# Queues, PSUM banks, tile places and the last block's weights, changed in a one-core encoder layer

## The chip, the core and the metric

The kernel runs on one NeuronCore of a Trainium2 chip. Five engines work beside each other, each through its own instructions in order: TensorE (PE in the profile; its weight loads are PEld), VectorE (DVE), ScalarE (ACT), GpSimd (POOL) and SyncE (SP), which here only issues DMAs. ACT and POOL can issue DMAs as well. The metric is the device time of one execution in microseconds.

## The reference

One inference step of a one-layer encoder in float32, for 2048 prompt tokens and 32 sample tokens, D_MODEL = 1024, D_FF = 4096:

```python
n = rmsnorm(x);  z = n @ w_in
A = sliding-window attention with sinks (8 heads of 64, window 128, chunks of 64)
B = gated linear attention (4 heads, dk 64, dv 128, state carried over chunks)
h = x + concat(A, B) @ w_out
y = h + relu(rmsnorm(h) @ w_up)**2 @ w_down
```

Outputs are y for both token sets, the last keys and values, and the GLA states.

## The kernel before

Every float32 operand is split into a high and a low float32r half, and a product is three matmuls (`mm3`: high by high, high by low, low by high). Tokens lie along the free axis, transposed, in chunks of 128.

**Attention** runs over 16 chunks and leaves its output of each chunk in a DRAM buffer `mixT` (the `aT` stores). **GLA** (gated linear attention) runs over the same chunks two at a time, with decay products `E` on POOL from a table `cc`, and puts its half into `mixT` (the `gT` stores). **The out-projection** (`op_phase`) takes the 2080 tokens as three pieces p of two groups gi, of 328 or 356 tokens a group: for each of eight feature blocks f, `op<-mx..,wo..` sums into PSUM, DVE adds the residual (tile y{p}{gi}, L1274), squares go into `acc` (L1277), and a matmul with ones (`oprb`) brings the token norm. The mix of a group is loaded from `mixT` and split into `mx0h`, `mx0l` or, for every other group, `mx1h`, `mx1l`.

**The FFN** is done by a Strassen-Winograd scheme: the matrices are cut in 2x2 quarters, and seven products take the place of eight. Its operands are sums of quarters. For tokens these are B11, B21, B22, T1 to T4, made by `post` in `op_phase` after a piece's second group and kept in DRAM as `Td`. For weights they are A11, A12, A22, S1 to S4, split in pairs on the fly by ACT (high) and DVE or POOL (low, L1380). The quarter sums of `w_down` (`sd`) are made by POOL in the phases before (L712) and stored: a unit is a load from `w_down`, some additions in place, and a store. EARLY blocks are made in the attention phase, in 4 parts each, in the two `cc` tiles that GLA uses later; MIDDLE blocks in GLA, the rest in `op_phase`. The three pieces run in the order 1, 2, 0. A piece has 16 blocks b of 256 of the 4096 features; a block has seven up steps (U, PSUM `u`) and seven down steps (D, PSUM `dn`), the D steps lagging behind the U steps, and the results are gathered in seven accumulators P1 to P7. The first piece also stores the sums of `w_up` (`su`) and the pairs of the first and last block (`ku`, `kd`), which the later pieces load. `prepare` makes weight pairs six steps ahead (AHEAD).

At a change of piece, the next piece's seven token operands are loaded and split, `load_tok`: a DMA into the low tile, ACT copies the high half, DVE or POOL subtract. These DMAs are ACT's; all others are SP's (queue Q, L59).

The order on each engine comes from a scheduler that runs over generators; their `yield n` are times on an estimated PE clock, which says when a piece of side work is offered. Each engine then runs its list in order. PSUM has eight banks: through the out-projection three for `oprb`, `opa`, `opb` and five for products; in the FFN, `ps2` holds two tiles of two banks for `dn`, and `ps1` the rest for `u`.

The lines that the prediction touches:

```python
S.dma_start(f32(l), self.Td[e.p][x])                       # load_tok
self.Q.dma_start(raw[:, k], w[b, :, k, :, c0 : c0 + n])    # load_block
Q.dma_start(self.mixT[t][:, 4:8, :], gT[:, :, :L])         # gla_phase
```

## Time and profile before

| | |
|---|---|
| Time, median of 3 runs | 2291.27 us (2290.83 to 2297.01) |
| Time of the profiled execution | 2295.51 us |
| Its span | 2293.6 us |
| Mean granted clock of TensorE | 0.968 |
| Busy: PE, DVE, ACT, POOL | 2155.3, 1575.3, 1232.0, 1474.0 us |
| Moved by DMA | 372.65 MB, 162 GB/s in the mean |

The phases in the profile: attention up to about 378 us, GLA to 745, the out-projection to 947, then the pieces of the FFN to about 1410, 1860 and the end. Busy time is read against what ended the idle time before an instruction: in `idle <-releaser` the releaser is the instruction or DMA whose semaphore came last. "SPq" and "ACTq" are the DMA issues of an engine's instruction list. PEclk is the TensorE clock that was granted, 1.00 being full speed.

### The profile page before, as it was taken

What the parts mean: (1) busy time and instruction counts of PE and PEld (TensorE: products, weight loads), DVE (VectorE), ACT (ScalarE), POOL (GpSimd) and SP (SyncE); (2) the same over time, 40 slices, a digit from 0 to 9 for tenths busy, and PEclk for the clock granted to TensorE, in tenths of its full rate; (3) what the DMA queues carried; (4) which work ended last, traced back from release to release, by engine and by line L of the source; (5) the groups of instructions that cost most, each with busy time, mean ns of one, the idle gap of its engine ahead of it and who ended that gap; (6) DMA issues with size and microseconds to landing.
All of it is one profiled execution on the core that took longest, in us unless ns stands there. A gap on an engine that the chain in (4) does not pass through costs nothing.

```text
span 2293.6 us, 40613 instructions
## 1 busy us (share of the span) xinstructions
PE 2155.3 (94%) x14790; PEld 2021.7 (88%) x14790; DVE 1575.3 (69%) x3442; ACT 1232.0 (54%) x2728; POOL 1474.0 (64%) x1324
## 2 busy tenths in 40 slices
PE   7999999799998599789999998999999989999997
PEld 6777777687887599789999998999999989999996
DVE  8766666688886445657777775576666666676667
ACT  4545455455563122456666665665565556666662
POOL 5233345343452453658878779978887889888884
PEclk9999999799998799899999999999999999999999
DMA  8344564251434875744444348544443475445433
GB/s 272 132 147 138 184 200 151 85 188 63 150 116 130 301 263 210 272 163 141 133 133 136 128 136 290 162 132 142 141 140 123 149 255 165 153 141 155 149 109 120
DMA packets 212729, 372.65 MB, mean 162 GB/s; under 512 B 43297, under 2 KB 140882, under 8 KB 207282
## 3 DMA queue, kind: packets, MB, share of 16 engines
q1 hardware_dynamic: 209506, 355.16, 47.0%
q10 hardware_dynamic: 3024, 14.91, 1.8%
q8 instruction: 116, 1.90, 0.3%
q14 instruction: 83, 0.68, 0.1%
HBM read 275.03 MB, written 94.98 MB: 161 GB/s over the span
## 4 chain that ended last, share of the span: by engine, by line
PE 52%; DMA 2%; DVE 2%; ACT 0%; issue 0%; POOL 0%; SPq 0%; ACTq 0%; DVEq 0%
PE dn L156 26%; PE u L156 26%; DVE P L1498 1%; DMA T3l<-Td2T 0%; DMA T1l<-Td2T 0%; DMA T1l<-Td0T 0%; DMA T2l<-Td0T 0%; DMA T3l<-Td0T 0%; DVE u L1498 0%; DMA B21l<-Td0B 0%; DMA T2l<-Td2T 0%; DVE P L1598 0%; SPq L59 0%; DMA stage<-sd 0%; DMA B11l<-Td2B 0%
## 5 line engine op out<-in xcount | busy, mean ns | idle before, releaser
L1498 DVE TENSOR_TENSOR P<-P,dn 128x712 f32<-128x712 f32 (+1 forms) x642 | 559.7, 875 | 234.5 <-PE dn L156 217.4
L43 ACT ACTIVATE u<-u 128x356 f32<-128x356 f32 (+1 forms) x384 | 174.0, 453 | 39.9 <-PE u L156 22.3
L43 ACT ACTIVATE r<-u 128x356 f32<-128x356 f32 (+1 forms) x192 | 88.6, 461 | 135.7 <-PE u L156 135.7
L1498 DVE TENSOR_TENSOR u<-u,r 128x356 f32<-128x356 f32 (+1 forms) x144 | 75.7, 526 | 122.5 <-PE u L156 117.6
L712 POOL TENSOR_TENSOR sd<-sd 128x128 f32<-128x128 f32 (+2 forms) x144 | 107.5, 761 | 75.1 <-DMA sd<-in_w_down 66.1
L945 POOL TENSOR_TENSOR E<-cc 128x256 f32<-128x256 f32 (+1 forms) x117 | 69.5, 628 | 103.2 <-DVE cc L797 49.0
L1405 POOL TENSOR_TENSOR stage<-stage 128x512 f32<-128x512 f32 x92 | 119.3, 1298 | 13.8 <-DMA stage<-in_w_up 8.3
L1021 DVE COPY_PREDICATED AT<-masks,A 64x64 f32<-64x64 int32 (+1 forms) x330 | 82.8, 253 | 22.3 <-ACT AT L43 13.0
L1598 POOL TENSOR_TENSOR P<-P,P 128x712 f32<-128x712 f32 (+1 forms) x38 | 65.0, 1732 | 21.8 <-DVE P L1498 21.6
L1274 DVE TENSOR_TENSOR y<-op,y 128x356 f32<-128x356 f32 (+1 forms) x48 | 23.5, 516 | 79.1 <-PE op L156 50.8
L43 ACT ACTIVATE P<-S,negm 128x192 f32<-128x192 f32 (+2 forms) x128 | 51.6, 417 | 46.7 <-DVE negm L577 38.4
L43 ACT ACTIVATE E<-E 128x1024 f32<-128x1024 f32 (+2 forms) x68 | 67.4, 1013 | 1.4 <-POOL E L937 0.3
L595 POOL TENSOR_TENSOR P<-P,es 128x512 f32<-128x512 f32 x15 | 16.0, 1065 | 74.2 <-ACT sq L43 44.4
L43 ACT ACTIVATE op<-y 128x356 f32<-128x356 f32 (+1 forms) x42 | 18.7, 464 | 76.0 <-DVE y L1274 67.6
L845 POOL TENSOR_TENSOR g<-g,ggla 128x512 f32<-128x512 f32 (+1 forms) x17 | 23.1, 1373 | 48.6 <-ACT g L43 48.6
L1498 DVE TENSOR_TENSOR u<-u,f 128x356 f32<-128x356 f32 (+1 forms) x96 | 49.9, 519 | 5.8 <-ACT u L43 5.7
L43 ACT ACTIVATE pS<-pT 128x256 f32<-128x256 f32 (+1 forms) x62 | 27.4, 490 | 48.9 <-PE pT L160 48.8
L956 DVE TENSOR_TENSOR E<-E,kq 128x256 f32<-128x256 f32 (+1 forms) x117 | 51.5, 496 | 1.5 <-ACT E L43 1.2
L576 DVE TENSOR_REDUCE mx<-S 128x2 f32<-128x384 f32 (+2 forms) x64 | 32.7, 535 | 28.6 <-PE S L156 28.4
L43 ACT ACTIVATE v<-go 128x256 f32<-128x256 f32 (+1 forms) x34 | 12.7, 380 | 73.5 <-DVE Sp L1053 46.0
L1281 POOL TENSOR_TENSOR z<-y 128x356 f32<-128x356 f32 (+1 forms) x12 | 11.8, 983 | 53.0 <-DVE y L1274 35.0
L43 ACT ACTIVATE f<-u 128x356 f32<-128x356 f32 (+1 forms) x96 | 43.7, 455 | 0.0
(1913 smaller groups left out, 8867.9 us busy)
## 6 DMA issues: line engine op xcount, KB each, us to landing
stage<-in_w_up SPq DMA_DIRECT2D x92, 512.0 KB, 3.9
stage<-sd SPq DMA_DIRECT2D x92, 512.0 KB, 4.4
stage<-in_w_down SPq DMA_DIRECT2D x46, 512.0 KB, 3.6
stage<-su SPq DMA_DIRECT2D x30, 512.0 KB, 3.9
stage<-in_w_down SPq DMA_DIRECT2D x46, 256.0 KB, 3.0
sd<-in_w_down SPq DMA_DIRECT2D x22, 512.0 KB, 5.6
sd<-sd SPq DMA_DIRECT2D x11, 1024.0 KB, 5.1
xT1a<-in_xT_prompt SPq DMA_DIRECT2D x16, 512.0 KB, 4.5
```

The lines of the kernel that those rows point to most:

```text
L43: ins = f(*args, **kw)
L156: self._pe(self.T.matmul(out, lhsT, rhs, start=start, stop=stop, **kw), ns)
L576: V.reduce_max(mx[:, ch, us], sp, axis=AX.X)
L712: self.G.tensor_tensor(out=o, in0=x, in1=y, op=op)
L845: G.tensor_tensor(out=gv, in0=gv, in1=ggla[:r].unsqueeze(1).broadcast_to([r, 4, P]), op=ALU.mult)
L945: G.tensor_tensor(out=e4, in0=c4, in1=ref, op=ALU.subtract)
L956: V.tensor_tensor(out=e4, in0=e4, in1=halves_of(kq, L, m), op=ALU.mult)
L1021: V.copy_predicated(dst, mk.unsqueeze(1).broadcast_to([L // nh, 2, w // m, m]), src[r].rearrange("s p (n m) -> s p n m", m=m),)
L1274: V.tensor_tensor(out=y[:, f], in0=ps, in1=y[:, f], op=ALU.add)
L1405: tt = lambda o, x, y, op: G.tensor_tensor(out=o, in0=x, in1=y, op=op)
L1498: add = lambda out, x, y, op=ALU.add: V.tensor_tensor(out=out, in0=x, in1=y, op=op)
L1598: eng.tensor_tensor(out=e.acc[q][:, j : j + 2], in0=e.acc[q][:, j : j + 2], in1=e.acc[x][:, j : j + 2], op=ALU.add)
```

## The change

Seven edits come together.

1. **Queues.** The stores of attention and GLA outputs, of the residual y and of the token operands go from SP's queue to ACT's, which makes their data last. The loads and stores of the weight sums, and the stores of kept sums and kept weight pairs, go from SP to POOL (G). The token loads go from ACT to SP; for the first piece five of the seven stay on ACT. The last piece's token stores stay on SP, cut in three by yields over the first four D steps.
2. **Token combinations.** `post` uses the PSUM tiles `rb` and `A` only; `B` is gone. The products of the out-projection get six banks. The FFN's `ps2` is cut in two pools, and the first four D steps of its first block use only the second, which does not lie over `rb` and `A`.
3. **Aligned tiles.** Paddings and the order of pools change, so that FFN tiles come to lie on single tiles of the out-projection: B11's high half on `mx0h`, the accumulators on y20, y21, z and the sums' tiles.
4. **EARLY** is 4 where it was 5; `op_phase` now makes seven blocks of sums.
5. **The last block's down pairs** are made and stored in blocks 9 to 12 of the first piece (`keep_last`), no longer in block 15. In block 14 the two pairs that DVE made are POOL's.

The core of the diff:

```diff
-EARLY, MIDDLE = 5, 5
+EARLY, MIDDLE = 4, 5
+PAD1, PADX = 164, 600
...
-                Q.dma_start(self.mixT[t][:, 4:8, :], gT[:, :, :L])
+                S.dma_start(self.mixT[t][:, 4:8, :], gT[:, :, :L])
...
-            self.Q.dma_start(raw[:, k], w[b, :, k, :, c0 : c0 + n])
+            self.G.dma_start(raw[:, k], w[b, :, k, :, c0 : c0 + n])
...
+            self.G.dma_start(self.sd[b][:, :, c0 : c0 + n], raw.rearrange("p k m n -> p (k m) n"))
             yield 6000
-            with self.tc.issue_after(self.Q.last.ins):
-                self.Q.dma_start(self.sd[b][:, :, c0 : c0 + n], raw.rearrange("p k m n -> p (k m) n"))
-            yield 8000
...
-            self.Q.dma_start(dst, x)
+            self.G.dma_start(dst, x)
...
+        pr, pp = pool("opr", 1, space=PSUM), pool("opp", 6, space=PSUM)
+        rb, pa = (pr.tile([P, 512], F32, tag=x, name=f"op{x}") for x in ("rb", "a"))
...
             for k in range(H):
                 scaled(A, k)
+                tt(y[:, k], A, y0[:, k])
                 scaled(y[:, H + k], H + k)
-                tt(t3[:, k], y[:, H + k], A)
-                tt(A, A, y0[:, k])
-                S.activation(y[:, k], A, AF.Copy)
-                tt(B, y[:, H + k], A)
-                S.activation(y0[:, k], B, AF.Copy)
-                tt(y0[:, H + k], y0[:, H + k], B)
+                tt(A, y[:, H + k], A)
+                S.activation(t3[:, k], A, AF.Copy)
+                tt(A, A, y0[:, k], ALU.add)
+                S.activation(y0[:, k], A, AF.Copy)
+                tt(y0[:, H + k], y0[:, H + k], A)
...
-            amem = {i: mem(pool(f"acc{i}"), H * NM, f"P{i}", F32) for i in (3, 5, 7, 6, 2, 4, 1)}
             umem["T4"] = upair(pool("ud"), "T4")
+            amem = {i: mem(pool(f"acc{i}"), H * NM, f"P{i}", F32) for i in (5, 7, 6, 2, 4, 1, 3)}
...
+            def keep_last(part):
+
+                b = NF - 1
+                if part == 0:
+                    s = load(w_dn[b, :, 0:1, :512], True)
+                    weights(f"d{b}A11", s, True, G)
+                    return
+                s = load(w_dn[b, :, 1:2, :] if part == 3 else self.sd[b][:, 2 * (part == 1) : 2 * (part == 1) + 2], True)
+                names = (("S4", "S1"), ("S2", "S3"), ("A12", "A22"))[part - 1]
+                cut = (s[:, :, :512], s[:, :, 512:]) if part == 3 else (s[:, 0:1], s[:, 1:2])
+                for x, src in zip(names, cut):
+                    weights(f"d{b}{x}", src, True, G)
...
-            def load_tok(e, x, engs):
+            def load_tok(e, x, engs, queue=Q):
 
                 h, l = e.T[x]
-                S.dma_start(f32(l), self.Td[e.p][x])
+                queue.dma_start(f32(l), self.Td[e.p][x])
...
-                    ps = ps2.tile([P, 2, 512], F32, tag="two", name=f"dn{g}_{q}_{j}")
+                    two = ps2[1] if g == 0 and i < 4 else ps2[j // 2]
+                    ps = two.tile([P, 2, 512], F32, tag="two", name=f"dn{g}_{q}_{j}")
...
+                    if n == 0 and 9 <= b < 13 and i == 3:
+                        keep_last(b - 9)
```

SP's list at the start of the out-projection, before (y01, y10 and y00 are residual tiles, `mixT` the mix, 128x8x40 is partitions by feature blocks by tokens):

```order
L59 DMA mixT15_81<-gT_15_9080 128x512
L59 DMA sd9_145<-sd9_0_8552 128x2048
L59 DMA y10_9263<-in_xT_prompt 128x8x128
L59 DMA y10_9263<-in_xT_prompt 128x8x84
L59 DMA y01_9214<-in_xT_prompt 128x8x88
L59 DMA y01_9214<-in_xT_prompt 128x8x128
L59 DMA y01_9214<-in_xT_prompt 128x8x112
L59 DMA m_4_112_9316<-mixT4_70 128x8x16
L59 DMA m_5_0_9320<-mixT5_71 128x1024
L59 DMA y00_9200<-in_xT_prompt 128x8x128 x2
L59 DMA y00_9200<-in_xT_prompt 128x8x40
L59 DMA y00_9200<-in_xT_sample 128x8x32
```

The loads of y00 are the last of the three residual tiles, behind the last `gT` store. After the change, SP's list in the middle of GLA (nTb, caf and g are loads of the next chunks of GLA):

```order
L60 DMA nTb_4h_5960<-nTh8_91 128x2048
L60 DMA nTb_4l_5961<-nTl8_92 128x2048
L60 DMA y00_9175<-in_xT_prompt 128x8x128
L60 DMA caf_4_6456<-ca8_109 96x128
L60 DMA g_7_6081<-rgd7_126 128x512
L60 DMA caf_4_6456<-ca9_110 96x128
L60 DMA y00_9175<-in_xT_prompt 128x8x128
L60 DMA y00_9175<-in_xT_prompt 128x8x40
L60 DMA y00_9175<-in_xT_sample 128x8x32
L60 DMA g_8_6615<-rgd8_127 128x512
L60 DMA rb_5_6485<-rs_118 128x128 x2
```

The loads of y00 moved from behind the last rows of GLA, and behind y10 and y01, to between the loads of the fourth pair of chunks.

DVE's list at the start of the FFN, before (opa and opb are the PSUM tiles of `post`, P3 and P5 accumulators, dn results of D steps):

```order
L1209 SCALAR_TENSOR_TENSOR opa_9198<-y21_10304,packed_211,oprb_9197 128x356
L1209 SCALAR_TENSOR_TENSOR y21_10304<-y21_10304,packed_211,oprb_9197 128x356
L1220 TENSOR_TENSOR y20_9883<-y20_9883,opb_9199 128x356
L1498 TENSOR_TENSOR uT4l_10827<-u0_0_10914,uT4h_10826 128x356
L1220 TENSOR_TENSOR T32_10718<-y21_10304,opa_9198 128x356
L1220 TENSOR_TENSOR opa_9198<-opa_9198,y20_9883 128x356
L1220 TENSOR_TENSOR opb_9199<-y21_10304,opa_9198 128x356
L1220 TENSOR_TENSOR y20_9883<-y20_9883,opb_9199 128x356
L1592 COPY P3_10798<-dn0_3_0_11169 128x712
L1592 COPY P3_10798<-dn0_3_2_11177 128x712
```

Both evacuations of P3 stand behind all of the combinations. After the change, the same list:

```order
L1220 TENSOR_TENSOR y20_9858<-y20_9858,opa_9146 128x356
L1615 COPY P3_10813<-dn0_3_0_11151 128x712
L1210 SCALAR_TENSOR_TENSOR opa_9146<-y21_10282,packed_211,oprb_9145 128x356
L1210 SCALAR_TENSOR_TENSOR y21_10282<-y21_10282,packed_211,oprb_9145 128x356
L1220 TENSOR_TENSOR y21_10282<-opa_9146,y20_9858 128x356
L1220 TENSOR_TENSOR opa_9146<-y21_10282,opa_9146 128x356
L1615 COPY P3_10813<-dn0_3_2_11159 128x712
L1390 TENSOR_TENSOR wf_d0A12_11215<-stage_11169,wf_d0A12_11215 128x512
L1220 TENSOR_TENSOR opa_9146<-opa_9146,y20_9858 128x356
```

The first evacuation by DVE, of P3, stood behind all combinations; it now stands ahead of the last one, and the second inside it.

More of the change, by code (lines that the diff above doesn't have):

```diff
@@ L1161, in op_phase @@
         nt, H = self.nt, KB // 2
+        pr, pp = pool("opr", 1, space=PSUM), pool("opp", 6, space=PSUM)
+        rb, pa = (pr.tile([P, 512], F32, tag=x, name=f"op{x}") for x in ("rb", "a"))
         m1 = pool("opm1", 1)
-        mem1 = [m1.tile([P, KB * REST + 272], F32R, tag=x, name=f"mx1{x}") for x in "hl"]
+        mem1 = [m1.tile([P, KB * REST + PAD1], F32R, tag=x, name=f"mx1{x}") for x in "hl"]
         m0 = pool("opm0", 1)
         mmem = [[m0.tile([P, KB * REST], F32R, tag=x, name=f"mx0{x}") for x in "hl"], mem1]
-        yps = [pool(f"opy{i}", 1) for i in (1, 2)]
-        tp, sp, xp = pool("opt", 1), pool("ops", 2), pool("opx", 3)
-        yps.insert(0, pool("opy0", 1))
+        sp, tp = pool("ops", 2), pool("opt", 1)
+        yps = [pool(f"opy{i}", 1) for i in (2, 1)]
+        xp = pool("opx", 3)
+        yps = [pool("opy0", 1), *yps[::-1]]
         stage = lambda name, n: tp.tile([P, H * REST], F32, tag="t", name=name)[:, : H * n].rearrange("p (k t) -> p k t", k=H)
-        rb, pa, pb = (self.ps_m(x) for x in ("oprb", "opa", "opb"))
         g = lambda f: self.gffn[:, f : f + 1]
@@ L1214, in post @@
                 yield
[L1215 to L1216 removed]
+                S.dma_start(Td["B11"], y[:, :H])
+                S.dma_start(Td["B21"], y[:, H:])
                 return
[L1218 to L1220 removed]
+            A, y0 = pa[:, :N], ys[p, 0]
+            tt = lambda o, x, z, op=ALU.subtract: V.tensor_tensor(out=o, in0=x, in1=z, op=op)
             for k in range(H):
                 scaled(A, k)
+                tt(y[:, k], A, y0[:, k])
                 scaled(y[:, H + k], H + k)
[L1224 to L1232 removed]
+                tt(A, y[:, H + k], A)
[3 more added lines that the diff above has]
+                tt(y0[:, H + k], y0[:, H + k], A)
+            last = p == 2
+            yield
+            eng = Q if last else S
+            eng.dma_start(Td["T3"], t3)
+            if last:
+                yield
+            eng.dma_start(Td["T1"], y[:, :H])
+            eng.dma_start(Td["B22"], y[:, H:])
+            if last:
+                yield
+            eng.dma_start(Td["T2"], y0[:, :H])
+            eng.dma_start(Td["T4"], y0[:, H:])
         mix = {(0, gi): self.mix[gi] for gi in range(2)}
@@ L1244, in begin @@
         def begin(b):
-            x = xp.tile([P, 2592], F32, tag="x", name=f"sd{b}")[:, :2048].rearrange("p (k m n) -> p k m n", k=2, m=2)
+            x = xp.tile([P, 2048 + PADX], F32, tag="x", name=f"sd{b}")[:, :2048].rearrange("p (k m n) -> p k m n", k=2, m=2)
             self.load_block(x, b, 0, 512)
@@ L1255, in end @@
         def end(b):
-            Q.dma_start(self.sd[b], sums.pop(b)[0].rearrange("p k m n -> p (k m) n"))
+            G.dma_start(self.sd[b], sums.pop(b)[0].rearrange("p k m n -> p (k m) n"))
         load_y(0, 0)
@@ L1268, in op_phase @@
                 else:
-                    ps = self.ps_s(f"op{p}_{gi}_{f}")[:, :N]
+                    ps = pp.tile([P, 512], F32, tag="op", name=f"op{p}_{gi}_{f}")[:, :N]
                     cs = slice(f % H * P, f % H * P + P)
@@ L1305, in ffn_phase @@
             pool = lambda name, **kw: ctx.enter_context(tc.tile_pool(name=name, bufs=kw.pop("bufs", 1), **kw))
-            ps2, ps1 = pool("ps2", bufs=2, space=PSUM), pool("ps1", space=PSUM)
+            ps2 = [pool(f"ps2{x}", space=PSUM) for x in "ab"]
+            ps1 = pool("ps1", space=PSUM)
             w_dn = a["w_down"].rearrange("(b k p) n -> b p k n", k=2, p=P)
@@ L1312, in ffn_phase @@
             tmem = tok(pool("toka"), ("T2", "T1"))
-            upair = lambda pool, x: [mem(pool, NM, f"u{x}{y}") for y in "hl"]
+            upair = lambda pool, x: [mem(pool, NM + 12 * (x + y == "B21h"), f"u{x}{y}") for y in "hl"]
             rf = pool("rf")
@@ L1465, in down_weights @@
                         src["A12"], src["A22"] = s[:, :, :512], s[:, :, 512:]
-                    eng = V if n == 0 and i in (0, 5) and not keep else G
-                    out[x] = weights(f"d{b}{x}", None if made else src[x], keep, eng)
+                    eng = V if n == 0 and i in (0, 5) and b < NF - 2 else G
+                    out[x] = weights(f"d{b}{x}", None if made else src[x], False, eng)
                     yield
@@ L1628, in ffn_phase @@
             for x, t in UP:
-                load_tok(envs[0], t, (V, G))
+                load_tok(envs[0], t, (V, G), Q if t in ("B11", "B21") else S)
             ups = {}
```

24 lines of the change are left out of this document (8 added, 16 removed).

## The prediction, made before the changed kernel ran

> **What bounds the kernel now.** I began with the busy shares and the clock row of the page.
>
> ```profile
> PE 2155.3 (94%) x14790; PEld 2021.7 (88%) x14790; DVE 1575.3 (69%) x3442; ACT 1232.0 (54%) x2728; POOL 1474.0 (64%) x1324
> PEclk9999999799998799899999999999999999999999
> ```
>
> TensorE (PE) is busy for 2155.3 of 2293.6 us, so 138 us of the span are idle on it. The change removes no matmul and keeps PE's order. It can only win idle time, and the part of the busy time that ran at a lowered clock. The waits of PE say where the idle time lies.
>
> ```profile
> PE oprb L156 <- issue: 21.1, 1, 21.1
> PE dn L156 <- DVE P L1498: 19.2, 9, 6.2
> PE dn L156 <- DVE y L1220: 13.1, 1, 13.1
> PE go L156 <- ACT cc L43: 9.8, 1, 9.8
> PE u L156 <- ACT B11h L43: 5.9, 1, 5.9
> PE op L156 <- POOL mx0l L1114: 5.8, 1, 5.8
> PE op L156 <- ACT mx0h L43: 2.9, 1, 2.9
> PE u L156 <- ACT r L43: 2.0, 1, 2.0
> PE dn L156 <- POOL wf_d0S L1380: 1.9, 1, 1.9
> PE u L156 <- DVE B11l L1496: 1.6, 1, 1.6
> ```
>
> (Columns: total us, times, longest.) They cluster at five joints: the start of GLA (`go`), of the out-projection (`oprb`, `op`), of the FFN (`u`, then `dn` behind `y`), and the two changes of piece. Inside a piece there is nothing to win. Each joint also lowers the clock behind it, which the windows show (columns after the name: length, then busy us of PE, PEld, DVE, ACT, POOL; PEclk; DMA share; GB/s).
>
> ```profile
> 421.00:430.00 9.00, 8.71 (x50) 6.67 (x51) 4.89 (x15) 7.90 (x17) 3.89 (x6) 0.52 0.17 46
> 771.00:778.00 7.00, 6.28 (x27) 6.31 (x28) 2.58 (x13) 0.00 (x0) 6.73 (x6) 0.51 0.88 315
> 800.00:812.00 12.00, 5.42 (x18) 5.18 (x19) 0.50 (x1) 4.15 (x7) 12.00 (x9) 0.57 0.86 255
> 947.00:959.00 12.00, 9.77 (x35) 8.90 (x36) 6.63 (x9) 4.73 (x8) 11.24 (x7) 0.51 1.02 418
> 982.00:987.00 5.00, 4.40 (x17) 4.43 (x18) 0.45 (x1) 1.36 (x2) 0.00 (x0) 0.59 1.02 418
> 1407.00:1413.00 6.00, 5.53 (x19) 5.53 (x20) 4.71 (x8) 3.86 (x8) 6.00 (x5) 0.52 0.75 298
> 1842.00:1847.00 5.00, 4.79 (x20) 4.79 (x21) 2.14 (x3) 0.16 (x1) 5.00 (x4) 0.66 0.92 359
> 1853.00:1857.00 4.00, 3.96 (x15) 3.50 (x15) 3.37 (x7) 3.42 (x8) 2.63 (x2) 0.57 1.05 411
> ```
>
> Busy time times (1 - clock) is what the clock cost: 4.2, 3.1, 2.3, 4.8, 1.8, 2.7, 1.6 and 1.7 us in turn. A joint's worth is its idle time plus this.
>
> **Start of GLA: 9.8 + 4.2 = 14.0 us.**
>
> ```profile
> 419.62 2.06 POOL L712 TENSOR_TENSOR sd<-sd 128x128 f32<-128x128 f32 x4 [1.93 <-DMA sd<-in_w_down]
> 420.39 0.84 ACT L43 ACTIVATE cc<-la,packed 128x256 f32<-128x256 f32 x2 [12.57 <-DMA sd<-sd]
> ```
>
> ACT cannot write `cc` until a store of early sums has left the same memory: the fifth early block is still being summed at 419.6. With EARLY at 4 no such block exists, and its work becomes a GLA unit with tiles of its own. I take 12 of the 14, since that unit now sits on POOL before the second group of decay products.
>
> **Start of the out-projection: 21.1 + 3.1 = 24.2 us.** PE stands before `oprb`, the token norm of group (0,0). DVE and SP tell why.
>
> ```profile
> DVE y L1274 <- DMA m<-mixT: 18.5, 1, 18.5
> DVE y L1274 <- DMA y<-in_xT_sample: 6.0, 1, 6.0
> 734.97 0.61 SPq L59 DMA_DIRECT2D mixT<-gT  x1
> 736.10 10.09 SPq L59 DMA_DIRECT2D y<-in_xT_prompt  x5
> ...
> 749.19 3.75 SPq L59 DMA_DIRECT2D y<-in_xT_prompt  x3
> 752.98 1.62 SPq L59 DMA_DIRECT2D y<-in_xT_sample  x1
> L1277 DVE TENSOR_TENSOR acc<-acc,op 128x328 f32<-128x328 f32 x8 | 9.8, 1236 | 0.6
> L1277 DVE TENSOR_TENSOR acc<-acc,op x42: 489/525/1375, 761.2 to 942.6; 128x356 f32<-128x356 f32 x28, 128x328 f32<-128x328 f32 x14
> ```
>
> The residual tile that group (0,0) adds to (y00) is loaded last, up to 752.98, behind the last `gT` store and the loads of two other groups. After the change its rows stand in GLA, and the `gT` stores are on ACT's queue. DVE can then finish the group as its products arrive. What stays is the `acc` chain: eight additions that took 1.24 us each here, between 745 and 780, against a median of 0.525 over all 42, while POOL made its sums. I leave 6 us of the 24.2 and take 18.
>
> The same stage then waits 2.9 + 5.8 us for `mx0h` and `mx0l` (worth 11.0 with the clock). Those loads still come off SP, DMA is 0.86 to 0.88 busy there, and POOL now issues 13 transfers ahead of the first `mx0l`. I take nothing.
>
> **Start of the FFN.** B11's tile (128544 to 134240 in a partition) lay over `mx1l`, the low half of the last group's mix; its new place is `mx0h`, free one group earlier. So 5.9 + 1.6 us idle and 4.8 of clock go: 12.3, of which I take 12. Next, `dn` waits 13.1 us because its banks were those of the combinations, and DVE finishes these first. In the change the first four down steps use one other buffer of two banks, so the first runs at once. Two prices stand against that. The third down result is evacuated by DVE in program order, behind three of the four combinations; and in one combination a PSUM tile serves where two did, so DVE waits for ACT's copies more often.
>
> ```profile
> L1220 DVE TENSOR_TENSOR opa<-opa,y x12: 501/532/533, 824.4 to 979.8; 128x356 f32<-128x356 f32 x8, 128x328 f32<-128x328 f32 x4
> L43 ACT ACTIVATE y<-opa x4: 467/468/477, 965.4 to 980.4; 128x356 f32<-128x356 f32 x4
> ```
>
> Two DVE subtractions hang on two ACT copies of 0.47 us each combination, some 1.0 us with the round trip left out, four times. DVE is late by 4 us there, and the single buffer costs an evacuation of under 1 us per step. I leave 8 of the 13.1, keep the clock loss, and take 5. From both sides: 13 if DVE is ahead, nothing if it isn't.
>
> **Changes of piece.** Here ACT issues each token load when its own order comes to it, and then stands still for the landing.
>
> ```profile
> 1392.21 0.80 ACT L43 ACTIVATE T1h<-T1l 128x712 fp32r<-128x712 f32 x1 [6.43 <-DMA T1l<-Td2T]
> 1392.22 0.36 ACTq L43 DMA_DIRECT2D T3l<-Td2T  x1
> 1400.56 1.49 ACT L43 ACTIVATE T3h<-T3l 128x712 fp32r<-128x712 f32 x2 [3.81 <-DMA T3l<-Td2T]
> 1332.00:1357.00 25.00, 25.00 (x156) 25.00 (x155) 19.64 (x29) 15.90 (x34) 19.42 (x16) 1.00 0.30 99
> 1382.00:1408.00 26.00, 17.16 (x103) 16.61 (x102) 12.16 (x19) 14.19 (x29) 26.00 (x18) 0.96 0.88 313
> ```
>
> Moving these loads to SP takes the 6.43 and 3.81 us out of ACT. Seven weight pairs of the last block and their stores leave the stretch 1382 to 1408, where POOL has no free time, for blocks 9 to 12, where it was busy 19.42 of 25 us. At the first change the waits are 2.65 and 6.2 (of the 19.2 above) and 1.9, with 2.7 of clock: 13.4, and I take 9. At the second they are 2.0, 2.85 and 1.17, with 3.3 of clock: 9.3, and I take 5, since no weights move there. SP now carries those loads among its weight loads; a load that waits for its tile holds the weights behind it, which is why I don't take all.
>
> **The issues themselves.** ACT's DMAs go from 21 to 64. At the 0.36 us of the rows above the 43 more take 15 us, spread over 950 us of an engine that is 54% busy, and behind work that the store needs anyway; I count nothing. Should ACT be late in GLA, where its order feeds the next chunk, these 15 us would be the most.
>
> 116 issues move to POOL. The trace of before has none from POOL, so I bound one: from below by ACT's 0.36 us, the same kind of instruction; from above by a whole transfer, since issuing cannot take longer than issue to landing.
>
> ```profile
> sd<-in_w_down SPq DMA_DIRECT2D x22, 512.0 KB, 5.6
> L1405 POOL TENSOR_TENSOR stage<-stage 128x512 f32<-128x512 f32 x92 | 119.3, 1298 | 13.8 <-DMA stage<-in_w_up 8.3
> ```
>
> The tightest place is blocks 9 to 12: 19.4 us of work in 25, plus 7/4 pairs of 1.30 us (2.3), plus 2.75 issues. At 0.36 us that is 22.7 us and nothing is late. At 2 us it is 27.2, and 4 x 2.2 = 9 us pile up, which the lead of six weight steps (6/14 of a block, 10.7 us) still hides. I take the low end, as the kind of instruction is the same, and 3 us for sums that now wait in POOL's order for loads issued just before them. The far end, 5.6 us, is a rival below. Block 14's two pairs that go from DVE to POOL (2.6 us) take the room that block 15's leave.
>
> The Trainium skill, page "SBUF — State Buffer", section "A bandwidth-pool intuition that's wrong (but worth ruling out)", says that a transfer issued from GpSimd takes about 0.62 us alone and 3.1 us beside a DVE copy that locks their shared port. No run here shows it yet. By 3.1 us the four blocks would be at 30.2 us, 21 us late in all, and the time some 17 us longer than my sum.
>
> **Sum.** 12 + 18 + 0 + 12 + 5 + 9 + 5 - 3 = 58 us. The profiled execution took 2295.5 us, which gives 2237.5. It lies 4.2 above the median 2291.27 of the runs shown (2290.83 to 2297.01), so for a median I forecast 2235 us.
>
> **Rivals.**
>
> *Half the joints stay* (22%). At the out-projection the transfers themselves may be the bound: DMA is at 0.88 there, and the tiles of four groups still have to arrive; at the FFN's start DVE's order holds `dn` as before. Then only GLA (12), B11 (12) and the changes of piece (14) pay: 38, less 3, so about 2257. Against it: the y00 rows move by a whole phase.
>
> *The wait moves into GLA* (8%). Row y00 on SP now waits until POOL has stored block 8's sums, and the next chunks' `caf` and `g` loads are queued behind it. If POOL gets there late, SP stalls in GLA and PE loses about what it won at the out-projection, 18 us with the clock: about 2253.
>
> *POOL's issues are dear: slower* (10%). The place is POOL before `mx0l` and in blocks 9 to 12, and c is the time of an issue.
>
> ```profile
> L712 POOL TENSOR_TENSOR sd<-sd 128x512 f32<-128x512 f32 x12 | 16.8, 1421 | 31.6 <-DMA sd<-in_w_down 31.4
> ```
>
> Between 745 and 780 POOL idles 31.6 us, so 13 issues are covered up to c = 2.4. In the four blocks the lag is 4 x (19.4 + 2.3 + 2.75c - 25), less 10.7 us of lead (six of the 14 steps of a 25 us block). At c = 4 these are 20 and 20 us, with about 12 of clock and as much again where early units crowd the attention phase; that eats the 58. From about 4 us an issue the kernel is slower; at 5 it is 33 + 31 + 14 + 20 - 58 = 40 us over, about 2335. Against it: POOL's issue would be ten times ACT's.
>
> The skill's figure of 3.1 us would fall short of that point.
>
> *Gains and costs cancel* (5%): c between 3 and 4, about 2288.
>
> **How the numbers follow.** The forecast, 55%, is 2235, with its own range 2215 to 2257 (every joint paid in full would be 2205). The range for 8 in 10 goes from 2207 to 2288. A measurement of this kernel tells 0.3%, 7 us, from no change. Faster: 55 + 22 + 8 = 85%, and 1 of the cancelling case, 86%; same 5%; slower 9%.
>
> **What would show it.** `go` no longer waits for `cc`; `oprb` waits under 8 us and DVE has no `y` wait for the sample rows; `u` has no wait for `B11h`; `dn` behind `y` is 8 us or less, with P3's evacuation as releaser; ACT has no wait of over 2 us for T1l or T3l. Idle PE time should fall from 138 to about 95 us. I am wrong if waits of PE for POOL's `E`, `P` or `wf_d` of blocks 9 to 13 grow, or if `op` waits longer for `mx0l` than 8.7 us.

## The result, and the profile after

| | before | after |
|---|---|---|
| Time, median of 20 runs | 2295.3 us | 2280.64 us |
| Ratio to before, 95% interval | 1 | 0.994 (0.9923 to 0.9957) |
| Span of the profiled execution | 2293.6 us | 2271.6 us |
| PE idle in it | 138 us | 116 us |

The kernel became faster by 0.6%, 14.7 us in the medians; the forecast was 58. One run of the kernel before took 2655.74 us, in a slower state, and is not in the ratio. The profiled execution of the changed kernel, 2273.34 us, is one of its faster ones, so its profile shows 22 us of gain.

The waits of PE after the change (total us, times, longest) have new entries in place of the old ones.

```profile
PE dn L157 <- DVE P L1520: 14.4, 9, 3.5
PE dn L157 <- DVE P L1615: 13.1, 4, 7.0
PE op L157 <- DVE y L1283: 8.3, 1, 8.3
PE go L157 <- ACT kdT L44: 6.8, 1, 6.8
...
PE op L157 <- POOL mx0l L1113: 4.7, 1, 4.7
PE oprb L157 <- DVE rsq_y_y L248: 4.4, 1, 4.4
PE op L157 <- ACT mx0h L44: 3.9, 1, 3.9
```

The waits for `cc`, for `oprb` at the start of the out-projection and for `B11h` are gone, 36.8 us in all. Each of the first four rows and the sixth holds something the forecast did not have.

PE runs the same list of matmuls in every version of this document, so the start of one matmul can be compared between profiles. The table gives, at the matmul that began at t in the profile before, how much later (+) or earlier (-) a version began it. The steps between columns are where a version wins or loses.

```text
t before (us)       120    400    460    540    740    785    940    970   1010   1270   1345   1450   1830   1910    end
after             +10.4   +3.4  -12.0   -7.9  -18.0  -41.3  -22.9  -39.1  -24.7  -25.1  -13.4  -22.6  -22.2  -24.7  -23.8
e1_no_keep        +11.8   +5.5   -7.8   -0.5  -10.3  -33.5  -12.4  -26.5  -10.1  -10.4  -10.6   -4.2   -4.8   -5.7   -4.6
e2_b11_pool        +9.6   +2.1  -13.7   -6.1  -16.9  -40.1  -18.0  -38.2  -24.1  -24.5  -13.4  -21.3  -21.5  -21.5  -20.6
e3_a_pool         +10.4   +4.9   -8.7   -4.2  -14.6  -37.5  -16.0  -31.7  -13.4  -13.8  -12.8  -17.8  -17.7  -17.1  -16.3
e4_tok_act         +8.8   +2.4  -11.2   -7.2  -16.9  -40.1  -19.6  -33.7  -17.1  -17.5   -7.9  -11.9  -12.6   -8.7   -8.6
e5_mid7            +8.7   +0.9  -13.5   -9.6  -16.3  -39.2  -25.5  -45.7  -29.2  -29.6  -21.2  -22.2  -22.2  -27.7  -27.7
e6_early5         +10.3   +1.2  -13.9   -9.5  -15.5  -38.8  -25.0  -39.1  -22.7  -23.1  -13.9  -17.8  -18.2  -20.1  -19.9
e7_sums_sp         +1.5   -4.6  -21.2  -26.0  -18.7  -39.4  -20.8  -38.4  -21.7  -22.1  -19.6  -29.8  -30.5  -30.9  -30.7
e8_no_align        +8.5   +2.6  -11.7   -4.8  -13.1  -36.3  -25.6  -37.3  -15.1  -15.1   -4.5   -3.5   -2.6   -3.4   -2.6
e9_comb            -0.0   -6.6  -20.0   -8.7  -10.1  -33.3  -20.1  -34.8  -20.8  -21.2  -19.6  -26.4  -27.1  -28.1  -27.2
e10_early_sp       +1.8   -5.7  -20.8   -8.7  -19.6  -42.4  -20.9  -34.0  -15.5  -15.9   -6.2  -11.4  -12.1  -13.8  -13.6
e11_late_y00      +12.4   +4.7  -11.1  -13.3  -24.5  -42.2  -21.0  -35.7  -21.9  -22.3  -12.4  -17.5  -18.2  -20.6  -20.4
e12_ps2            +9.8   +4.4   -9.3   -3.1  -13.8  -36.6  -14.6  -21.7  -20.9  -21.3  -11.0  -13.1  -13.8  -19.6  -19.4
e13_three          +1.3   -6.0  -21.0  -20.4  -32.3  -49.6  -34.0  -49.0  -35.7  -36.1  -35.5  -40.8  -40.4  -44.9  -44.7
e14_early5_three   +1.7   -3.9   -4.3   -3.8  -12.9  -32.3  -14.4  -28.0  -11.5  -11.9  -12.2  -17.4  -18.1  -18.8  -17.9
e15_no_es          +8.4   +2.1  -11.8  -11.5  -22.3  -39.7  -24.9  -37.2  -22.4  -22.8  -21.8  -24.3  -23.8  -24.9  -24.7
```

Row "after" in steps: 10 us lost at the start of attention and mostly regained by 400; 15 won at the start of GLA (400 to 460); 4 lost and 10 won inside it (460 to 540, 540 to 740); 23 won at the start of the out-projection (740 to 785) and 18 lost inside it (785 to 940); 16 won and 14 lost again at the start of the FFN; 12 lost in blocks 11 and 12 of the first piece (1270 to 1345); 9 won and 2 won at the changes of piece. Four places gave back what the joints had won. One lies in each of the next four timelines.

Each row is one execution, so a step is only as sure as it repeats. Up to 1214 us the lists of all engines are the same in "after", e1, e3 and e4, whose edits touch later blocks only. These four win 22.8 to 23.3 us at the start of the out-projection and lose 18.4 to 21.5 inside it, but from 940 to 1010 one wins 1.8 and three lose 2.3 to 2.6, and at 940 their sums stand 10 us apart.

**Blocks 11 and 12.** DVE, then POOL, then PE, in the changed kernel:

```profile
1267.19 0.88 DVE L1520 TENSOR_TENSOR P<-P,dn 128x712 f32<-128x712 f32 x1
1267.99 6.12 DVE L1390 TENSOR_TENSOR wf_d11A<-stage,wf_d11A 128x512 fp32r<-128x512 f32 x1
1274.47 1.68 DVE L1520 TENSOR_TENSOR P<-P,dn 128x712 f32<-128x712 f32 x2
...
1267.34 1.28 POOL L1390 TENSOR_TENSOR wf_d11S<-stage,wf_d11S 128x512 fp32r<-128x512 f32 x1
1268.59 1.27 POOL L1390 TENSOR_TENSOR wf_u12S<-stage,wf_u12S 128x512 fp32r<-128x512 f32 x1
1269.83 1.27 POOL L1415 TENSOR_TENSOR s<-stage 128x512 f32<-128x512 f32 x1
1271.07 1.27 POOL L1390 TENSOR_TENSOR wf_u12S<-stage,wf_u12S 128x512 fp32r<-128x512 f32 x1
1272.31 1.25 POOL L1415 TENSOR_TENSOR stage<-stage 128x512 f32<-128x512 f32 x1
...
1275.41 0.43 PE L157 MATMUL dn<-uT3h,wf_d11S 128*128 128x356 f32 x1 [3.33 <-DVE P L1520]
```

A subtraction that takes 0.68 us elsewhere (both operands in SBUF) lasts 6.12 us, until half a microsecond after POOL's gapless run ends at 1273.6. The accumulation behind it is late, and PE waits. Block 12 shows the same at 1300. The accumulations `P<-P,dn`, with one operand in PSUM, are not slowed beside POOL.

**Inside the out-projection**, DVE waits for a residual tile. The window (columns as in the prediction's) shows the DMA engines full meanwhile (share 1.05, 353 GB/s).

```profile
833.89 2.70 DVE L1283 TENSOR_TENSOR y<-op,y 128x356 f32<-128x356 f32 x6 [15.40 <-DMA y<-in_xT_prompt]
800.00:832.00 32.00, 26.17 (x167) 25.87 (x166) 7.33 (x23) 3.25 (x5) 14.91 (x11) 0.96 1.05 353
```

**At the FFN's start** the first `dn` no longer waits long, but the third accumulator's evacuation waits for a store: P5's new place is the tile of T3.

```profile
964.37 0.90 DVE L1615 COPY P<-dn 128x712 f32<-128x712 f32 x1 [3.83 <-DMA Td2T<-T]
956.48 0.93 SPq L60 DMA_DIRECT2D Td2T<-T  x1
```

**In GLA**, SP waits 10.2 us for a store of sums before it can load y00, and GLA's own `g` load is queued behind; ACT then waits for `g`.

```profile
SPq L60 <- DMA sd<-sd: 10.2, 1, 10.2
496.10 0.62 SPq L60 DMA_DIRECT2D y<-in_xT_prompt  x1
497.91 0.33 SPq L60 DMA_DIRECT2D g<-rgd  x1
501.58 0.63 ACT L44 ACTIVATE g<-g 128x512 f32<-128x512 f32 x1 [5.79 <-DMA g<-rgd]
503.96 0.79 PE L157 MATMUL go<-Sp,Qc 64*128 64x128 f32 x2 [6.80 <-ACT kdT L44]
```

### The profile page after: what moved, and what is told of

The parts are those of the page before. It is cut to its first block, busy times and chain, and to the rows that moved or that the text cites. A ratio compares the mean times of both kernels' runs of the same rounds, so it can differ in the third digit from the quotient of the medians.

```text
span 2271.6 us, 40566 instructions
## 1 busy us (share of the span) xinstructions
PE 2156.1 (95%) x14790; PEld 2023.4 (89%) x14790; DVE 1586.8 (70%) x3440; ACT 1232.3 (54%) x2728; POOL 1537.3 (68%) x1430
## 4 chain that ended last, share of the span: by engine, by line
PE 80%; DVE 7%; DMA 5%; POOL 3%; issue 3%; ACT 2%; SPq 1%; DVEq 0%; ACTq 0%; POOLq 0%
PE dn L157 26%; PE u L157 26%; PE op L157 7%; PE zq L157 5%; PE zv L157 3%; PE zr L157 3%; PE zkv L157 2%; PE zk L157 2%; PE go L157 1%; PE O L157 1%; PE A L157 1%; DVE P L1520 1%; PE S L157 1%; SPq L60 1%; PE pT L161 1%
## 5 line engine op out<-in xcount | busy, mean ns | idle before, releaser
L713 POOL TENSOR_TENSOR sd<-sd 128x128 f32<-128x128 f32 (+2 forms) x132 | 101.1, 782 | 29.2 <-DMA sd<-in_w_down 26.6
L720 POOL DMA_DIRECT2D sd<-in_w_down x56 | 36.3, 652 | 15.6 <-DMA sd<-sd 10.5
L577 DVE TENSOR_REDUCE mx<-S 128x2 f32<-128x384 f32 (+2 forms) x64 | 32.8, 535 | 16.9 <-PE S L157 16.6
L1647 POOL TENSOR_TENSOR P<-P,stage 128x712 f32<-128x712 f32 (+1 forms) x24 | 41.5, 1729 | 1.5 <-DVE P L1520 1.5
```

What stands on the lines that cost most here:

```text
L577: V.reduce_max(mx[:, ch, us], sp, axis=AX.X)
L713: self.G.tensor_tensor(out=o, in0=x, in1=y, op=op)
L720: self.G.dma_start(raw[:, k], w[b, :, k, :, c0 : c0 + n])
L1647: G.tensor_tensor(out=at, in0=at, in1=waiting.pop(g), op=ALU.add)
```

## The experiments

Each starts from the changed kernel. Ratios are to the kernel before, with 95% intervals; the changed kernel's is 0.994 (0.9923 to 0.9957). The kernel before ran again beside each version, the changed kernel did not: where the intervals overlap, the times don't tell a version from the changed kernel.

### e1_no_keep: the last block's pairs in block 15 again

```diff
+                keep = b == NF - 1
-                    eng = V if n == 0 and i in (0, 5) and b < NF - 2 else G
+                    eng = V if n == 0 and i in (0, 5) and not keep else G
-                    if n == 0 and 9 <= b < 13 and i == 3:
-                        keep_last(b - 9)
```

> The changed kernel with the last block's weight pairs made in block 15 again, and block 14's two pairs on DVE (all else as changed). Theory PORT: in the changed kernel's profile one DVE subtraction in each of blocks 11 and 12 took 6.12 us, where 0.68 is the least, because it reads two operands from SBUF while POOL runs five such operations without a gap; PE then waits 3.3 us each time and loses 1.7 and 3.1 us of clock, and the curve of PE's start times falls 11.8 us behind there. Without the extra work on POOL no such subtraction takes over 1.8 us and these 11.8 us come back; the change of piece at about 1390 loses at most the 9 us that it had won. Net against the changed kernel: 12 to 3 us faster. Theory PLACE (the prediction): blocks 9 to 12 have room, the two waits have another cause, and the move is worth most of the 9 us at the change of piece: 5 to 9 us slower than the changed kernel, waits in blocks 11 and 12 as before.

Ratio 0.9935 (0.9909 to 0.9962): no difference from the changed kernel. DVE's subtractions in blocks 11 and 12 are short again (min/median/max in ns):

```profile
L1390 DVE TENSOR_TENSOR wf_d11A<-stage,wf_d11A x2: 685/906/1126, 1261.8 to 1281.6; 128x512 fp32r<-128x512 f32 x2
L1390 DVE TENSOR_TENSOR wf_d12A<-stage,wf_d12A x2: 686/901/1116, 1289.1 to 1308.9; 128x512 fp32r<-128x512 f32 x2
```

From 1270 to 1345 nothing is lost, where the changed kernel loses 11.7. From 1345 to 1450 it loses 6.4 where the changed kernel wins 9.2. The move costs 12 us in the blocks that it moved to. At the change of piece it is worth 15 by these two rows, but the versions that keep it and keep the token loads on SP lie there between a loss of 1.0 (e8) and a win of 10.2 (e7): 5 to 17 us.

### e3_a_pool: the held subtractions given to POOL

```diff
-                    eng = V if n == 0 and i in (0, 5) and b < NF - 2 else G
+                    eng = V if n == 0 and i in (0, 5) and b < 10 else G
```

> The changed kernel with the two DVE subtractions of blocks 10 to 13 (pairs A11 and A12 of the down weights) given to POOL. Theory PORT: the 6.12 us operations are gone from DVE, PE's waits for P in blocks 11 and 12 fall under 1 us, and up to 11.8 us come back, less what POOL loses through 2 x 1.3 us more in each block. Theory FULL (POOL is simply over its time in these blocks, and the low halves come late): POOL's lag grows by 10 us over the four blocks, PE waits for weights of blocks 12 to 14, and the time is 5 to 15 us longer than the changed kernel's.

Ratio 0.9881 (0.9845 to 0.9917), faster than the changed kernel. The two windows of 60 us around blocks 11 and 12, of the changed kernel and of this one:

```profile
1255.00:1315.00 60.00, 53.12 (x298) 52.23 (x297) 45.49 (x55) 32.02 (x70) 45.84 (x40) 0.91 0.43 143
```

```profile
1262.00:1322.00 60.00, 60.00 (x372) 60.00 (x372) 41.00 (x62) 37.25 (x80) 56.40 (x49) 1.00 0.55 183
```

POOL now works 56.4 of 60 us, against 45.8, and PE never waits. POOL's load was not what hurt; DVE's operation held up by POOL's was. This tells PORT from FULL.

### e2_b11_pool: B11's and B21's low halves on POOL

```diff
-                load_tok(envs[0], t, (V, G), Q if t in ("B11", "B21") else S)
+                load_tok(envs[0], t, (G,) if t in ("B11", "B21") else (V, G), Q if t in ("B11", "B21") else S)
```

> The changed kernel with the low halves of B11 and B21 of the first piece made wholly on POOL (half of each was DVE's). In the changed kernel DVE's half of B11l took 4.97 us (888.4 to 893.4; the same shape takes 0.90 when nothing holds it) in the middle of the token norm of group (2,0), and PE then waited 4.4 us for that norm, with 3.2 us of clock behind it. Theory PORT: the wait falls under 1 us and 5 to 7.6 us come back by 940. Theory ORDER: the norm is late for another reason (its own place in DVE's list, the late y rows), the wait stays at 3 us or more, and POOL's two added operations of 1.7 us can only delay the FFN's first product.

Ratio 0.9918 (0.9885 to 0.995), not told apart from the changed kernel. In the changed kernel's profile DVE's half had taken 4.97 us beside a gapless run of POOL and ended when POOL issued a DMA:

```profile
888.40 4.97 DVE L1518 TENSOR_TENSOR B11l<-B11l,B11h 128x712 fp32r<-128x712 f32 x1 [1.13 <-ACT B11h L44]
...
888.44 1.30 POOL L1415 TENSOR_TENSOR stage<-stage 128x512 f32<-128x512 f32 x1
889.70 1.26 POOL L1415 TENSOR_TENSOR s<-stage 128x512 f32<-128x512 f32 x1
890.93 1.68 POOL L1518 TENSOR_TENSOR B11l<-B11l,B11h 128x712 fp32r<-128x712 f32 x1
892.55 0.56 POOL L1393 DMA_DIRECT2D ku0S<-wf_u0S  x1
```

Here the wait for the norm is gone: against the changed kernel, 7 us are won on PE's curve at 925. Right after, 12 us are lost, for group (2,1)'s residual tile:

```profile
PE op L157 <- DVE y L1283: 17.7, 2, 9.3
```

There are two such waits now, where there was one. But e1, e3 and e4, with the changed kernel's lists here, also wait twice (16.5 to 17.0 us) and not for the norm. In them DVE's half took 0.91 to 1.00 us. It began about 0.3 us before POOL's next operation, and then that one was late (1.79 us for 1.30). From e1:

```profile
894.52 0.91 DVE L1519 TENSOR_TENSOR B11l<-B11l,B11h 128x712 fp32r<-128x712 f32 x1 [0.91 <-ACT B11h L44]
894.78 1.79 POOL L1415 TENSOR_TENSOR stage<-stage 128x512 f32<-128x512 f32 x1
```

In the changed kernel's profile the two began within 0.04 us of each other, and DVE was held. So PORT holds for the operation, but the hold-up belongs to that execution, and this edit can't show what its removal is worth. In all four versions without it a transfer is late behind it.

### e4_tok_act: the token loads of pieces two and three on ACT again

```diff
-            def load_tok(e, x, engs, queue=Q):
+            def load_tok(e, x, engs, queue=S):
```

> The changed kernel with the token loads of the second and third piece issued by ACT again. The prediction put 9 + 5 us on the changes of piece, from ACT no longer issuing these loads in its own order: then ACT waits 4 to 6 us for T1l and T3l again, and 8 to 14 us are lost at the two changes. Rival: at the first change of piece the gain came from the weight pairs that left it; then under 4 us are lost in all.

Ratio 0.9957 (0.9937 to 0.9976); the intervals overlap. The curve wins 4.0 us at the first change and loses 3.9 at the second, where the changed kernel wins 9.2 and 2.5. The versions that leave these loads and pairs as changed lie between -1.0 and +10.2 at the first and between -0.6 and +5.8 at the second. So a loss, of 3 to 10 us, is shown at the second change alone. ACT's waits there:

```profile
ACT T1h L44 <- DMA T1l<-Td0T: 7.4, 1, 7.4
ACT T2h L44 <- DMA T2l<-Td0T: 3.8, 1, 3.8
```

With e1, which loses 6.4 us at the first change, that one owed more to the weight pairs than to the loads.

### e5_mid7 and e6_early5: fewer sums in the out-projection

```diff
-EARLY, MIDDLE = 4, 5
+EARLY, MIDDLE = 4, 7
```

> The changed kernel with two more blocks of weight sums made in GLA (7 for 5), so that the out-projection makes five and not seven. Theory DMA: after the change the out-projection is bound by its transfers (the DMA engines are 0.99 busy from 800 to 832 us at 317 GB/s, and DVE waits 15.4 us for the residual tile of group (1,1)). 4 MB leave that stage, about 13 us at 317 GB/s: PE's waits for y there (8 to 17 us in the profiles so far) shrink by 6 to 13 us and the kernel is that much faster than the changed one. Theory ORDER: the tile is late because of its place in SP's list, behind the tile of group (2,0); the waits stay within 2 us, and so does the time. Either way GLA may lose up to 4 us to POOL's added sums.

Ratio 0.9902 (0.9871 to 0.9933). From 785 to 940 it loses 13.7 us and not 18.4; PE's wait for the tile of group (1,1) falls from 8.3 to 2.2 us. (The window of the changed kernel shown above has a DMA share of 1.05 and 353 GB/s, not the 0.99 and 317 of the expectation.)

```profile
828.63 0.57 PE L157 MATMUL op<-mx1h,wo10h 128*128 128x356 f32 x1 [2.18 <-DVE y L1283]
904.87 0.67 PE L157 MATMUL op<-mx1h,wo10h 128*128 128x356 f32 x1 [8.37 <-DVE y L1283]
```

The wait at 905, for group (2,1)'s tile, stays: that load starts after the stores of the piece before have left its memory, and lands among them.

```diff
-EARLY, MIDDLE = 4, 5
+EARLY, MIDDLE = 5, 5
```

> The changed kernel with five early blocks of sums again, so that the out-projection makes six. The prediction's first step put 12 us on this part alone, at the start of GLA: then PE waits about 10 us for cc there, and the curve of its start times loses 12 to 14 us by 440. With 2 MB less in the out-projection, theory DMA gives 6 us back there (net 6 to 8 us slower than the changed kernel); theory ORDER gives nothing back (12 to 14 us slower). Rival to the step itself: with sums on POOL's queue the early stores land in time and cc doesn't wait; then no loss at 420.

Ratio 0.9906 (0.9869 to 0.9943). There is no wait for `cc` at all: 15.1 us are won from 400 to 460, as in the changed kernel. With sums on POOL's queue the fifth early block is stored in time. The out-projection, with 2 MB less, loses 13.8 and not 18.4. By itself EARLY at 4 wins nothing here and costs some 5 us on the curve; the ratio can't confirm that. Theory DMA holds for group (1,1) in both runs: PE's wait for that tile is 6.0 to 9.0 us in the versions with seven blocks, 3.4 here and 2.2 with five.

### e7_sums_sp and e10_early_sp: sums back on SP's queue

e7 gives back all of POOL's DMAs but the store of z; e10 only the sums of the attention phase.

```diff
-            self.G.dma_start(raw[:, k], w[b, :, k, :, c0 : c0 + n])
+            self.Q.dma_start(raw[:, k], w[b, :, k, :, c0 : c0 + n])
...
-            self.G.dma_start(dst, x)
+            self.Q.dma_start(dst, x)
```

> The changed kernel with the loads and stores of weight sums and the stores of kept sums and pairs on SP's queue again. The changed kernel's profile shows 0.56 us of POOL for such an issue, 65 us in all for 116. The prediction took 3 us for them. If POOL's part is as cheap as forecast, the time stays within 6 us of the changed kernel, and what SP regains in waits shows in late weights. Rival: the 8 to 10 us that the changed kernel loses in the first 120 us come from POOL's issues ahead of the first low halves, and return with this edit.

Ratio 0.9888 (0.985 to 0.9925). By 120 it has regained 8.9 us of the changed kernel's 10.4, by 540 it is 18 us ahead of it, and by 740 all of that is lost in GLA, where SP's list is the long one: it loses 7.3 from 540 to 740, where the changed kernel wins 10.1, and `dk` waits 12.1 us for `AT` in all, against 2.9 there and 9.0 before. The ratio is nevertheless better than the changed kernel's, at the edge of what can be told. Blocks 11 and 12 lose only 2.5 us; DVE's subtractions are held there for 4.2 and 5.0 us. Why for less than 6.1 stays open.

```diff
+            q = self.Q if b < EARLY else self.G
-            self.load_block(raw, b, c0, n)
+            self.load_block(raw, b, c0, n, q)
```

> The changed kernel with the loads and stores of the attention phase's sums alone on SP again. The changed kernel falls 8 to 10 us behind the one before in the first 120 us of PE's start times. If POOL's place (four issues of 0.7 us, and sums that wait in its list ahead of the first low halves) is the cause, 8 us come back by 120; of these 3 to 5 may be lost again at 280 to 360, where the kernel before waited for POOL. If the cause is another (ACT's stores, weight loads further behind in SP's list), nothing comes back.

Ratio 0.9924 (0.9896 to 0.9953). The 8.6 us by 120 come back, and are lost at 500, where `kdT` now waits 9.3 us: an early PE only meets y00's load sooner. POOL's first rows in the changed kernel, then a row of ACT, and SP's row from before, show what was late first:

```profile
1.97 3.05 POOL L720 DMA_DIRECT2D sd<-in_w_down  x4
8.73 0.99 POOL L713 TENSOR_TENSOR sd<-sd 128x128 f32<-128x128 f32 x2 [3.71 <-DMA sd<-in_w_down]
12.27 2.35 POOL L271 TENSOR_TENSOR wq1l<-stage,wq1h 128x1024 fp32r<-128x1024 f32 x1 [2.55 <-ACT wq1h L44]
11.14 1.06 ACT L44 ACTIVATE wq1h<-stage 128x1024 fp32r<-128x1024 f32 x1 [0.89 <-DMA stage<-in_w_in]
...
4.55 2.67 SPq L59 DMA_DIRECT2D sd<-in_w_down  x4
```

`wq1l` began at 10.09 before. The sums ahead of it in POOL's list are not what holds it: it waits for ACT's `wq1h`, and that for its weights. The loads of the sums now start at 1.97, beside SP's weight loads, and no longer at 4.55 behind them. The curve has regained these 2 us by 25; it then loses 6 from 25 to 35, 2 from 60 to 70 and 2 from 100 to 110. So e10 shows that the early sums' DMAs on POOL cost 8.6 us; which of their effects costs it is not shown.

### e8_no_align: the old places

```diff
-PAD1, PADX = 164, 600
+PAD1, PADX = 272, 544
...
+            amem = {i: mem(pool(f"acc{i}"), H * NM, f"P{i}", F32) for i in (3, 5, 7, 6, 2, 4, 1)}
-            amem = {i: mem(pool(f"acc{i}"), H * NM, f"P{i}", F32) for i in (5, 7, 6, 2, 4, 1, 3)}
```

> The changed kernel with the paddings and the pools' order of before, so that B11's high half lies on the last group's mix again and the accumulators on other tiles. The prediction put 12 us on B11's place. If that holds, PE waits 6 us or more for B11h at the FFN's start, with about 4 us of clock, and the start is 10 to 12 us later. Against it stands the wait of 7.0 us for P5 in the changed kernel (its new place is T3's, which must be stored first): where that goes with the old places, 7 to 9 us come back. Net within 5 us of the changed kernel if both hold; 12 slower if only the first; 9 faster if only the second.

Ratio 0.9966 (0.9944 to 0.9989). The wait for `B11h` is back, and the old places are worse for the accumulators too. In the out-projection, though, PE waits for one residual tile, where e1, with the aligned places, waits for two (last two rows, e8 and e1):

```profile
PE dn L157 <- DVE P L1614: 16.4, 2, 15.4
PE u L157 <- ACT B11h L44: 6.5, 1, 6.5
PE op L157 <- DVE y L1282: 8.5, 1, 8.5
PE op L157 <- DVE y L1283: 17.0, 2, 8.6
```

From 940 to 1010 it wins nothing, and loses 10.5; the changed kernel wins 1.8, and e1, e3 and e4 lose 2.3 to 2.6. The aligned places are worth 8 to 12 us at this joint, about what was forecast for B11 alone, though two waits make up the sum. But from 785 to 940 the old places lose 10.7 us, the aligned ones in these four profiles 18.4 to 21.5. From 785 to 1010 together it is 21.2 against 16.6 to 24.1, and the ratios overlap: a gain of the aligned places over both stages is not shown.

### e11_late_y00: the first residual tile loaded behind GLA

```diff
-        load_y(0, 0)
+        with tc.issue_after(self.state_out.ins):
+            load_y(0, 0)
```

> The changed kernel with the residual tile of group (0,0) loaded behind GLA's last rows of SP's list, as before the change (but ahead of the tiles of the other groups). The prediction put 18 us on its early load. If so, PE stands 10 us or more at oprb near 740 and 14 to 20 us are lost by 780. Rival: with the gT stores off SP's list the tile arrives in time even here, and under 5 us are lost; then the early place is not what won.

Ratio 0.991 (0.988 to 0.9939). PE waits 2.4 us for the norm where it had waited 21.1, and the curve wins 17.7 from 740 to 785. So the early place was not needed: with the sums and the `gT` stores off SP's list, and y00 first of the three tiles, a late load arrives in time. The early place does win 5.6 us more here (23.3). But from 460 to 540 the late one wins 2.2 where the changed kernel loses 4.1, and from 460 to 785 together it wins 31.1 against 29.3. Which of the three, the sums, the `gT` stores or the order of the tiles, makes the late load land in time is not separated.

### e12_ps2: both PSUM pools from the first down step on

```diff
-                    two = ps2[1] if g == 0 and i < 4 else ps2[j // 2]
+                    two = ps2[j // 2]
```

> The changed kernel with the first four down steps of the FFN using both PSUM pools, so that the first one needs the banks of the token combinations. The prediction put 5 us on avoiding that. If it holds, PE stands 10 us or more before the first dn (it stood 13.1 before the change) and 3 to 8 us are lost there. Rival: the down steps wait for the accumulators' tiles (stores of the last piece's token operands) in any case, as the 7.0 us for P5 say; then the wait only moves to the first dn, and the time stays within 3 us.

Ratio 0.9914 (0.9884 to 0.9943). PE stands 10.6 us before the first `dn` again:

```profile
PE dn L157 <- DVE y L1220: 10.6, 1, 10.6
```

Yet from 940 to 1010 it wins 6.3 us, where the changed kernel wins 1.8: the later waits for P (L1615) have shrunk to 4.8 us from 13.1. That fits the rival: the start of the FFN is bound by the last combinations and their stores, and the banks only decide where PE stands.

### e9_comb, e13_three, e14_early5_three and e15_no_es: the readings together

e9 has e3, e5 and e10 together. e13 has e3, e10 and e11 (their three edits, nothing else); e14 adds EARLY = 5 to e13, with the fifth block on POOL; e15 is e14 with all sums on POOL.

> The changed kernel with three edits together: A11 and A12 of the down weights of blocks 10 to 13 made on POOL, two more blocks of sums in GLA (7 for 5), and the sums of the attention phase loaded and stored by SP again, as before the change. If the three readings hold and add up (12 us in blocks 11 and 12, 7 us at the out-projection's group (1,1), 5 to 9 us in the attention phase), the span is 2243 to 2252 us against 2271.6 of the changed kernel, a ratio of about 0.982 to before. If the gains only move waits on to transfers that are late anyway, it stays over 2262 us (0.987 or more).

Ratio 0.9859 (0.983 to 0.9888), between its two bounds: from 530 to 560 it loses 7 us where the changed kernel wins 7, and PE waits 19.7 us for `AT` in all. POOL's added sums in GLA are the likely cause; no run takes them alone.

> The changed kernel with A11 and A12 of blocks 10 to 13 on POOL, the attention phase's sums on SP, and y00's load behind GLA's rows; sums as in the change (4 early, 5 in GLA, 7 in the out-projection). Readings so far: 12 us in blocks 11 and 12, 8.6 in the attention phase, 6 to 9 at 500 where GLA's g load waits behind y00. If they are separate causes, PE's curve is 20 us or more ahead of the changed kernel's at 740 less what GLA takes back, no wait for P in blocks 11 and 12, and the ratio is 0.983 to 0.986. If GLA takes back whatever the attention phase wins (it did in three runs), the ratio is 0.987 to 0.990 with only blocks 11 and 12 won.

Ratio **0.9832 (0.9803 to 0.9862)**, median 2254.65 us: faster than both kernels, and what was expected if the causes are separate. The attention phase's gain lasts through GLA, since y00 no longer stands in the way (-20.4 at 540, against -8.7 in e10), and blocks 11 and 12 lose 0.6 us.

> The same with five early blocks (the fifth on POOL), so that the out-projection makes six and not seven. If the out-projection is bound by its transfers, its wait at group (1,1) falls by 5 to 8 us against the run with four, and the ratio is 0.980 to 0.984. If the fifth early block delays cc at the start of GLA again, 8 to 14 us are lost at 420 and the ratio is 0.986 or more.

Ratio 0.9923 (0.9899 to 0.9947). The wait for `cc` is back:

```profile
ACT cc L44 <- DMA sd<-sd: 9.5, 1, 9.5
PE go L157 <- ACT cc L44: 7.0, 1, 7.0
```

From 400 to 460 it wins 0.4 us, e13 15.0. So EARLY at 4 is worth 15 us where the early sums are SP's, and nothing where they are POOL's (e6). The wait for group (1,1)'s tile falls from 6.0 us (e13) to 3.8, less than the 5 to 8 us expected.

> The same as the run with five early blocks, with all sums on POOL's queue as in the change. What the attention phase wins with its sums on SP (8.6 us by 120) is missing at 120; if GLA takes that back anyway, the two end within 4 us of each other, and if not, this one is 6 to 9 us slower.

Ratio 0.9865 (0.9834 to 0.9895): not slower than e14 but faster, since with the sums on POOL the wait for `cc` does not come back.

## Why the prediction was wrong

- **Start of GLA** (12): right in size, 15 us, but for one of two reasons. e6 and e14 show that either the smaller EARLY or POOL's queue removes the wait.
- **Start of the out-projection** (18): 23 us, and the cause I gave was a part of it. e11 wins 17.7 with y00 loaded late. The early place wins 5.6 more here and costs about as much in GLA: the rival "the wait moves into GLA" was real beside the gain (6.8 us of wait at 504, e10 and e11), though I had made them alternatives.
- **Inside the out-projection** (0): this is the largest miss, 18 us. I took nothing for the stage's transfers and put "half the joints stay" at 22%. PE came 41 us earlier to a stage that DMA fills (share 1.05 from 800 to 832), and waited there 8.3 us for a residual tile and 4.4 for a norm; in e1, e3 and e4 it waited for two tiles, 16.5 to 17.0. EARLY at 4 also put a seventh block, 2 MB, into it; I had not counted the DMAs of that step. e5, with 4 MB less, loses 13.7. So 5 us of the 18 are shown to come from those bytes; the wait for the second tile (8.4 us) stays there, and that the stage's other transfers cause it is argued from its load alone.
- **FFN's start** (12 + 5): B11's wait went as said (e8), but the joint won 2 us, and in e1, e3 and e4 it lost 2. The step that failed is the price of the single buffer and of DVE's order, where I left 8 of the 13.1 us and put no further wait behind them: it did not see that P5's new place must first be stored, nor the clock lost again (0.77 granted from 956 to 968 us). e12 has the old banks and loses nothing by it. The new places also come with a second late tile in the out-projection (e8).
- **Changes of piece** (9 + 5): 9 and 2.5 in the changed kernel's profile, but a loss of 1 to a win of 10 at the first one in others that leave it as changed. There the pairs mattered more than the loads (e1, e4).
- **Blocks 9 to 12** (0): 12 us lost. PE's waits for `P` there grew from none to 6.9 us, which I had named as a sign of being wrong. I checked whether POOL had time for the work, and it had: e3 gave it more and gained. What failed was the step that named POOL's idle time as the only cover. POOL's gaps also let DVE's two-operand subtractions in, and the moved work closed them. The row of 1.24 us for `acc`, which I quoted, was a sign: group (0,0)'s `op` lies in SBUF, and POOL ran beside it.
- **POOL's issues** (3): an issue takes 0.53 to 0.88 us, well under the 4 us of the rival of dear issues. The early sums on POOL still cost: 10 us are lost by 120, 8.6 of them to these DMAs (e10), and 3 remain at 400. That sums wait in POOL's order, as I had it, is not shown to be the reason. My bound was also misread: of POOL's 31.6 idle us, which I put between 745 and 780, some 18 lie in that window, so 13 issues were covered up to 1.4 us each, not 2.4.
- **Inside GLA** (not in the sum): 4 lost and 10 won, the latter by the sums' new queue (e7).

The parts that I called rivals were not exclusive: the joints did pay, and the waits that take their place came as well. That 2281 lies near the 2288 of the rival "Gains and costs cancel" is chance, since that one rests on issues of 3 to 4 us.

## What to carry to other kernels

When a stall is removed ahead of a stage that DMA fills, count that stage's bytes at the new, earlier time before taking the gain, the loads and stores of every step that the change adds to it included. Free time on POOL is also DVE's chance to run subtractions with both operands in SBUF; before work is moved there, look for such operations of DVE beside it and what they hold up. A load put early into a list in order can wait for its memory and hold back the loads behind it, so test the late place too. And before a step of one profile is given a cause, look whether it repeats in another execution of the same list.
